# Even attention: the two softmaxes of a block joined on GpSimd in three operations, and a head's six epsilons in one

## The chip, the cores and the metric

The kernel runs on one core of a Trainium2 chip. The core has a matrix engine, TensorE (PE in the profile), which writes to PSUM; VectorE (DVE); ScalarE (ACT); and GpSimd (POOL), which reads and writes SBUF and not PSUM. SyncE (SP) issues most of the DMAs. Each engine works through its own instructions in a fixed order and waits on semaphores for the others. The metric is the device time of one execution in microseconds. The kernel before takes 1602.63 us, the median of three runs (1602.38 to 1602.99).

## What is computed

Two transformer layers over 512 tokens and 256 context tokens, width 1024, in fp32. The first layer's mixer ("even") is a gated chunk MLP beside a differential attention; the second's is a windowed attention with sinks; a SwiGLU follows each. The change lies in the differential attention, in which each of four heads has two sets of queries and keys of width 64 and values of width 128:

```python
def diff_attn(q, k, v, lam):
    ...
    s = jnp.einsum('bqhd,bkhd->bhqk', q, k).astype(jnp.float32) * ATTN_SCALE
    p = jax.nn.softmax(s, axis=-1).reshape(b, B_HEADS, 2, tq, tk)
    a = p[:, :, 0] - lam * p[:, :, 1]
    return jnp.einsum('bhqk,bkhe->bqhe', a.astype(v.dtype), v)

def diff_out(o, g, lam_init):
    b, t = o.shape[0], o.shape[1]
    return (rmsnorm(o, g) * (1.0 - lam_init)).reshape(b, t, B_V_WIDTH)
```

Token queries see all 768 keys, context queries only the 256 context keys. Since an RMS norm over the head's output follows, the kernel never divides by the first softmax's sum s0: it forms e0 - lam (s0 / s1) e1 from the two arrays of exponentials and their row sums s0 and s1, and puts EPS s0^2 into the norm in place of EPS.

## The kernel before

Matrices are split into a high and a low part ("hi", "lo") so that three fast matmuls make one of fp32 accuracy (`mm3`, L106 to L108). ScalarE makes the high part, VectorE or GpSimd subtracts it for the low one (`split`, L122 and L123; for weights `unit`, L81 and L84).

The even attention goes head by head, t = 0 to 3. `head(t)` calls `attend` for three pairs of blocks of 128 queries, qp = 0, 1, 2; the first two pairs are token queries with 768 keys ("long blocks"), the third is context queries with 256 ("short blocks"). `attend` calls `softmax_diff` for both blocks, then PE transposes the two joined arrays 128 columns at a time (L564), ScalarE and VectorE split them (L122, L123), three matmuls each multiply them with the values (L106 to L108), and ScalarE copies the output (L576).

In `softmax_diff`, for each of the two softmaxes c: scores on PE into a PSUM tile pw (L542, L543; two such tiles exist), the negated row maximum on VectorE (L544), the exponential with its row sum on ScalarE (L546) into an SBUF tile e (six exist). Then VectorE takes the reciprocal of s1 (L550), the factor -lam s0 / s1 (L551), the join e0 + factor e1 into e0 (L552), and the block's epsilon EPS s0^2 (L553).

Beside this, `head` does the previous head's norm in three steps (`norm`; the diagonal scalings are L173, the spreading matmuls L183, the product L609) and, in qp 1, stacks the next head's Q and K into hi and lo (`stack`: L261 and L262 on ScalarE and L265 for Q, L276 and L277 on ScalarE and L279 for K; L265 of the last head is on GpSimd, all other subtractions on VectorE).

Between the heads' matmuls PE has those of `gated(i)`, eight dense products for the gated MLP, into one PSUM tile pf, which ScalarE empties (L585). Their weights come through a ring: DMA by SyncE, high part on ScalarE (L81), low part on GpSimd (L84). In order of priority stand heads 0 and 1, then heads 2 and 3, with gated 4 to 7 and then `turn` and gated 0 to 3 behind them. The gelus of gated 4 to 7 (L632) stand on ScalarE behind the last exponential of head 1, and heads 2 and 3 on ScalarE behind these gelus; each change between the two functions costs a table load.

The order of the instructions on each engine isn't written by hand. The context `tile.TileContext(nc, schedule_with_timeline_sim=True)` plans it at build time from priorities and its own costs, and sets all semaphores. `issue_after` puts an instruction behind another one on the same engine.

Of the kernel before, what the change touches and what calls it, by code (L numbers as in the profile page):

```python
# [11 lines left out]
ALU = mybir.AluOpType  # L12
# [10 lines left out]
EPS = 1e-6  # L23
# [3 lines left out]
class Builder:  # L27
# [294 lines left out]
    def even(self):  # L322
        tc, nc, a = self.tc, self.nc, self.a
# [7 lines left out]
        def f3(tag="f3", bufs=8):  # L331
            return R1.tile([P, TA], F32, name=self.uid(tag), tag=tag, bufs=bufs)
# [4 lines left out]
        for k in range(0, KT, 2):  # L337
            t = self.load(Rh, a["xT"][k * P:(k + 2) * P, :].rearrange("(k p) t -> p k t", p=P), [P, 2, TX], f"hx{k}")
# [110 lines left out]
        for half, heads in enumerate(((0, 1), (2, 3))):  # L449
# [3 lines left out]
            for k in range(KT):  # L453
                t = self.adap.tile([P, 2, 512], F32R, name=self.uid("wq"), tag="wq", bufs=3) if k % 3 == 2 else None
# [8 lines left out]
                if half == 0:  # L463
                    t, sh = hx[k], self.modcol(0, 0, k, 0)
# [35 lines left out]
        for k in range(KT):  # L500
            W = self.unit(a["v0"][k * P:(k + 1) * P, :], 512)
            for tb in range(6):
                c = slice(tb * P, (tb + 1) * P)
# [24 lines left out]
        Ra = tc.alloc_tile_pool(name="att0", bufs=1, side="right", reuse_waits="tile")  # L528
        oraw, raw = [], {}

        def softmax_diff(Q, K, qb, eps):


            koff = 0 if qb < 4 else TX
            qs = slice(qb * P, (qb + 1) * P)
            nm, sums = self.small(2, "sa", 10), self.small(2, "sa", 10)
            es = []
            for c in range(2):
                ps = self.wide()
                for p in range(2):  # L540
                    if qb < 4:
                        nc.tensor.matmul(ps[:, :TX], Q[c][:, qs], K[c][p][:, :TX], start=p == 0, stop=p == 1)  # L542
                    nc.tensor.matmul(ps[:, TX:TA], Q[c][:, qs], K[c][p][:, TX:], start=p == 0, stop=p == 1)  # L543
                nc.vector.tensor_reduce(nm[:, c:c + 1], ps[:, koff:TA], axis=AX, op=ALU.max, negate=True)  # L544
                e = Ra.tile([P, TA], F32, name=self.uid("e"), tag="e", bufs=6)
                self.last_exp = nc.scalar.activation(e[:, koff:], ps[:, koff:TA], AF.Exp, bias=nm[:, c:c + 1],  # L546
                                                     accum_out=sums[:, c:c + 1])
                es.append(e[:, koff:])
            r = self.small(1, "sa", 10)
            nc.vector.reciprocal(r, sums[:, 1:2])  # L550
            nc.vector.scalar_tensor_tensor(r, r, self.nlam, sums[:, 0:1], ALU.mult, ALU.mult)  # L551
            nc.vector.scalar_tensor_tensor(es[0], es[1], r, es[0], ALU.mult, ALU.add)  # L552
            nc.vector.scalar_tensor_tensor(eps[:, qb:qb + 1], sums[:, 0:1], EPS, sums[:, 0:1], ALU.mult, ALU.mult)  # L553
            return es[0]

        def attend(t, Q, K, qp, o, eps):
            es = [softmax_diff(Q, K, 2 * qp + i, eps) for i in range(2)]
            kbs = list(range(6)) if qp < 2 else [4, 5]
            po = self.bank()[:, :TC]
            for i in range(0, len(kbs), 2):  # L560
                pt = self.bank()
                for j in range(2):
                    for b in range(2):
                        nc.tensor.transpose(pt[:, j * TC + b * P:j * TC + (b + 1) * P],  # L564
                                            es[b][:, (i + j) * P:(i + j + 1) * P], self.ident)
                th = Ra.tile([P, 512], F32R, name=self.uid("ath"), tag="at", bufs=6)
                tl = Ra.tile([P, 512], F32R, name=self.uid("atl"), tag="at", bufs=6)
                self.split(th, tl, pt)
                for j in range(2):
                    kb = kbs[i + j]  # L570
                    c = slice(t * P, (t + 1) * P)
                    m = slice(j * TC, (j + 1) * TC)
                    self.mm3(po, (vhi[kb][:, c], vlo[kb][:, c]), (th[:, m], tl[:, m]),
                             i + j == 0, i + j == len(kbs) - 1)
            s = slice(qp * TC, (qp + 1) * TC)
            nc.scalar.copy(o[:, s], po)  # L576
# [11 lines left out]
        def stack(t):  # L588
            return (self.stack_q(qk[t], Ra, TA, "sq", 3, eng=nc.gpsimd if t == 3 else nc.vector),
                    self.stack_k(qk[4 + t], Ra, TA, "sk", 6))  # L590
# [3 lines left out]
        def norm(t, step):  # L594

            if t not in norms:
                return
            o, eps = norms[t][:2]
            if step == 0:
                sq = self.sumsq()  # L600
                nc.scalar.activation(sq, o, AF.Square)
                norms[t] = o, eps, sq
            elif step == 1:
                sq = norms[t][2]
                norms[t] = o, eps, self.rstd_diag([(sq[:, :TX], TX), (sq[:, TX:], TC)], 1.0 / P, eps=eps)
            else:
                for off, T, dg in ((0, TX, norms[t][2][0]), (TX, TC, norms[t][2][1])):
                    c = o[:, off:off + T]
                    nc.vector.scalar_tensor_tensor(c, c, self.subg, self.spread(dg), ALU.mult, ALU.mult)  # L609

        def head(t):
            Q, K = QK.pop(t)
            o = f3("o", 4)
            eps = self.small(6, "sx", 2)
            for qp in range(3):
                attend(t, Q, K, qp, o, eps)
                if qp == 0:
                    norm(t - 1, 1)
                elif qp == 1:
                    if t < 3:  # L620
                        QK[t + 1] = stack(t + 1)
                    norm(t - 1, 2)
            norms[t] = o, eps
            norm(t, 0)
            if t == 3:
                norm(t, 1)
                norm(t, 2)
            oraw.append(o)
# [40 lines left out]
        for t in range(2):  # L669
            head(t)  # L670
# [5 lines left out]
        with tc.high_priority(offset=tc.cur_priority - here), tc.issue_after(last.ins):  # L676
            head(2)
            head(3)
# [889 lines left out]
```

## Time and profile before

| | us |
|---|---|
| median of three runs | 1602.63 |
| the profiled execution | 1600.63 |
| its span | 1598.8 |
| PE busy | 1522.4 |
| DVE busy | 1066.6 |
| POOL busy | 833.9 |
| ACT busy | 724.5 |

The profile shows one execution. Its span runs from the first to the last instruction of the trace; the rest of its time lies around that. Times of a trace are microseconds from the span's start. The four heads of the even attention run from 168 to 304 us; the rest of the span lies outside what is edited.

How lines are read: a group has line, engine, operation, out<-in, shapes and count, then busy time and mean nanoseconds of one, then the idle time of the engine just before them and what ended it. In a view of one line the three numbers are shortest, median and longest. In the chain of work that ended last each piece is followed back to what released it, so that the shares by line show what set the time; "issue" is time in which the engine waited for nothing that the profile shows. PEclk is the clock that TensorE was granted, as a share of the full one.

### The profile page before, as it was taken

Reading aid. Unit: us, or ns where it says so; the run is one execution under the profiler, and the core shown is the slowest. Engines: PE = TensorE matmul, PEld = TensorE weight load, DVE = VectorE, ACT = ScalarE, POOL = GpSimd, SP = SyncE. Lnnn points to the kernel's source line nnn. Section 1 sums busy time; section 2 is a strip of 40 time slices with the busy share of each in tenths; the row PEclk is TensorE's granted clock in tenths of the full one; section 3 lists DMA queues with packets and bytes.
Section 4 is the critical chain, followed back from the end, with each engine's and each line's share of the span. In section 5 each row is a group of like instructions: output and inputs, shape, how many; then the busy total and the mean of one; then the engine's idle time right before and its main releaser. Section 6 shows DMA issues by size and latency. Waiting matters only on the chain.

```text
span 1598.8 us, 24991 instructions
## 1 busy us (share of the span) xinstructions
PE 1522.4 (95%) x9547; PEld 1356.4 (85%) x9547; DVE 1066.6 (67%) x1956; ACT 724.5 (45%) x1472; POOL 833.9 (52%) x567
## 2 busy tenths in 40 slices
PE   6999988999989999999999989999999899999996
PEld 4676876889989999999999978777869899999996
DVE  4620788765687787878774485665667866666656
ACT  2422676553543333333333244565655645444442
POOL 0463211061256776777676415541304399888883
PEclk9999999999999999999999999999999999999998
DMA  8845100033233333454541012110225132323201
GB/s 326 306 139 191 40 8 1 14 127 124 67 98 107 112 99 123 153 156 147 162 156 48 27 52 80 60 34 14 67 80 204 52 111 97 113 86 113 93 14 54
DMA packets 54296, 162.01 MB, mean 101 GB/s; under 512 B 6176, under 2 KB 10656, under 8 KB 46496
## 3 DMA queue, kind: packets, MB, share of 16 engines
q1 hardware_dynamic: 47120, 135.11, 25.1%
q10 hardware_dynamic: 7056, 25.30, 5.0%
q8 instruction: 75, 1.23, 0.3%
q14 instruction: 45, 0.37, 0.1%
HBM read 158.29 MB, written 2.10 MB: 100 GB/s over the span
## 4 chain that ended last, share of the span: by engine, by line
PE 84%; DVE 9%; ACT 4%; issue 2%; DMA 1%; POOL 0%; POOLq 0%; SPq 0%; DVEq 0%; ACTq 0%
PE pw L107 11%; PE pw L106 11%; PE pw L108 11%; PE pb L107 8%; PE pb L106 8%; PE pb L108 8%; PE pf L106 4%; PE pf L107 4%; PE pf L108 4%; PE pb L1421 2%; PE pb L1410 2%; PE pf L359 2%; PE pw L1373 1%; PE pw L1381 1%; PE pw L542 1%
## 5 line engine op out<-in xcount | busy, mean ns | idle before, releaser
L84 POOL TENSOR_TENSOR w<-raw,w 128x512 fp32r<-128x512 f32 (+1 forms) x84 | 126.8, 1517 | 244.0 <-ACT w L81 221.9
L107 PE MATMUL pw<-ax,w 128*128 128x384 f32 (+2 forms) x732 | 234.0, 320 | 5.2 <-DVE ax L201 2.7
L774 DVE SCALAR_TENSOR_TENSOR xT<-pb,mod,xT 128x512 f32<-128x512 f32 (+3 forms) x208 | 146.0, 707 | 133.2 <-PE pb L108 132.7
L106 PE MATMUL pw<-ax,w 128*128 128x384 f32 (+2 forms) x732 | 232.7, 321 | 2.1 <-ACT ax L200 1.6
L108 PE MATMUL pw<-ax,w 128*128 128x384 f32 (+2 forms) x732 | 233.4, 320 | 0.1
L879 POOL TENSOR_TENSOR w<-t,w 128x512 fp32r<-128x512 f32 x100 | 152.8, 1531 | 58.8 <-ACT w L879 56.9
L879 POOL TENSOR_TENSOR w<-raw,w 128x512 fp32r<-128x512 f32 x110 | 166.6, 1530 | 23.3 <-ACT w L879 23.2
L106 PE MATMUL pb<-hh,w 128*128 128x512 f32 x480 | 171.3, 357 | 3.5 <-DVE xT L774 3.5
L108 PE MATMUL pb<-hh,w 128*128 128x512 f32 x480 | 171.7, 358 | 0.0
L107 PE MATMUL pb<-hh,w 128*128 128x512 f32 x480 | 171.3, 357 | 0.0
L106 PE MATMUL pw<-T,w 128*128 128x384 f32 (+1 forms) x508 | 157.0, 311 | 2.1 <-DVE hs L879 2.1
L107 PE MATMUL pw<-T,w 128*128 128x384 f32 (+1 forms) x508 | 157.7, 311 | 1.2 <-DVE T L123 1.2
L108 PE MATMUL pw<-T,w 128*128 128x384 f32 (+1 forms) x508 | 157.7, 311 | 0.0
L106 PE MATMUL pf<-ax,w 128*128 128x256 f32 (+2 forms) x420 | 140.4, 334 | 10.2 <-DVE qf L252 5.7
L107 PEld LDWEIGHTS pw<-ax,w 128*128 128x128 f32 x732 | 139.3, 190 | 12.5 <-DVE ax L201 3.6
L106 PEld LDWEIGHTS pw<-ax,w 128*128 128x128 f32 x732 | 138.7, 190 | 9.8 <-ACT ax L200 2.4
L108 PE MATMUL pf<-ax,w 128*128 128x256 f32 (+2 forms) x420 | 139.6, 332 | 3.2 <-DVE w L879 3.2
L108 PEld LDWEIGHTS pw<-ax,w 128*128 128x128 f32 x732 | 139.5, 191 | 3.1 <-DVE w L948 0.4
L107 PE MATMUL pf<-ax,w 128*128 128x256 f32 (+2 forms) x420 | 139.1, 331 | 0.0
L879 POOL TENSOR_TENSOR w<-rawo,w 128x512 fp32r<-128x512 f32 x60 | 104.9, 1749 | 32.6 <-ACT w L879 26.1
L879 POOL TENSOR_TENSOR hh<-hs,hh 128x512 fp32r<-128x512 f32 (+1 forms) x41 | 76.7, 1873 | 85.3 <-ACT hh L879 83.9
L228 DVE SCALAR_TENSOR_TENSOR junk<-ar,cb 128x1024 bf16<-128x1024 f32 x64 | 105.0, 1641 | 1.5 <-DMA ar<-ada 1.5
(380 smaller groups left out, 3926.1 us busy)
## 6 DMA issues: line engine op xcount, KB each, us to landing
raw<-ffn_in SPq DMA_DIRECT2D x44, 1024.0 KB, 5.2
ar<-ada SPq DMA_DIRECT2D x24, 1024.0 KB, 7.1
ar<-ada ACTq DMA_DIRECT2D x48, 512.0 KB, 3.6
rawo<-ffn_out SPq DMA_DIRECT2D x88, 256.0 KB, 3.0
raw<-odd_out SPq DMA_DIRECT2D x32, 256.0 KB, 2.7
raw<-qk SPq DMA_DIRECT2D x16, 256.0 KB, 8.5
raw<-uv SPq DMA_DIRECT2D x16, 256.0 KB, 2.8
raw<-even_out SPq DMA_DIRECT2D x8, 512.0 KB, 4.1
```

The source lines that it names most:

```text
L84: eng.tensor_tensor(lo, raw, hi.bitcast(F32), ALU.subtract)
L106: mm(out, s[0], m[0], start=start, stop=False, **kw)
L107: mm(out, s[0], m[1], start=False, stop=False, **kw)
L108: return mm(out, s[1], m[0], start=False, stop=stop, **kw)
L228: return self.nc.vector.scalar_tensor_tensor(junk, t, 1.0, self.cb[who], ALU.mult, ALU.mult, accum_out=self.acc[who][:, col:col + 1])
L359: nc.tensor.matmul(ps[32 * q:32 * q + 32, :w], cst[:, k, :], t[:, w * q:w * q + w], start=k == 0, stop=k == KT - 1, skip_group_check=True)
L542: nc.tensor.matmul(ps[:, :TX], Q[c][:, qs], K[c][p][:, :TX], start=p == 0, stop=p == 1)
L774: ins = self.nc.vector.scalar_tensor_tensor(h, ps[:, r], self.modcol(l, j, m, who), h, ALU.mult, ALU.add)
L879: tail[key] = fn(*args, **kw)
L1373: nc.tensor.matmul(ps[:, st:en], Q, K[g][p][:, b0 * P:b1 * P], start=p == 0, stop=p == 1, skip_group_check=True)
L1410: last = nc.tensor.transpose(pt[:, x * P:(x + 1) * P], es[2 * (x % 2) + x // 2][:, kb * P:(kb + 1) * P], self.ident)
L1421: nc.tensor.matmul(po[64 * h:64 * h + 64, :], V[vb][:, 64 * g:64 * g + 64], t[:, h * TC:h * TC + TC], start=kb == 0, stop=kb == nb - 1, sk ...
```

## The change

```diff
-        def softmax_diff(Q, K, qb, eps):
+        def softmax_diff(Q, K, qb, s0):
...
-            nm, sums = self.small(2, "sa", 10), self.small(2, "sa", 10)
+            nm, s1 = self.small(2, "sa", 10), self.small(1, "sa", 10)
+            sums = [s0[:, qb:qb + 1], s1]
...
                 self.last_exp = nc.scalar.activation(e[:, koff:], ps[:, koff:TA], AF.Exp, bias=nm[:, c:c + 1],
-                                                     accum_out=sums[:, c:c + 1])
+                                                     accum_out=sums[c])
                 es.append(e[:, koff:])
             r = self.small(1, "sa", 10)
-            nc.vector.reciprocal(r, sums[:, 1:2])
-            nc.vector.scalar_tensor_tensor(r, r, self.nlam, sums[:, 0:1], ALU.mult, ALU.mult)
-            nc.vector.scalar_tensor_tensor(es[0], es[1], r, es[0], ALU.mult, ALU.add)
-            nc.vector.scalar_tensor_tensor(eps[:, qb:qb + 1], sums[:, 0:1], EPS, sums[:, 0:1], ALU.mult, ALU.mult)
+            po = nc.gpsimd
+            nc.vector.reciprocal(r, s1)
+            po.tensor_scalar(r, r, self.nlam, sums[0], ALU.mult, ALU.mult)
+            po.tensor_scalar(es[1], es[1], r, None, ALU.mult)
+            po.tensor_tensor(es[0], es[0], es[1], ALU.add)
             return es[0]
...
         def head(t):
             Q, K = QK.pop(t)
             o = f3("o", 4)
-            eps = self.small(6, "sx", 2)
+            s0, eps = self.small(6, "sx", 4), self.small(6, "sx", 4)
             for qp in range(3):
-                attend(t, Q, K, qp, o, eps)
+                attend(t, Q, K, qp, o, s0)
...
+            nc.vector.scalar_tensor_tensor(eps, s0, EPS, s0, ALU.mult, ALU.mult)
             norms[t] = o, eps
```

The reciprocal of s1 stays on VectorE. The factor, the product of the second array with it (written in place) and the sum are three operations of GpSimd, where one operation of VectorE made the factor and one the join. The first softmaxes' sums of a head's six blocks are written by ScalarE side by side into one tile s0, a column each; behind the head's last block one VectorE operation makes all six epsilons from it.

## The prediction

> **What bounds the kernel now.** The page comes first. TensorE (PE) is busy nearly the whole span, the chain of work that ended last runs 84% over it, and VectorE (DVE) stands next with 9%.
>
> ```profile
> span 1598.8 us, 24991 instructions
> ...
> PE 1522.4 (95%) x9547; PEld 1356.4 (85%) x9547; DVE 1066.6 (67%) x1956; ACT 724.5 (45%) x1472; POOL 833.9 (52%) x567
> ...
> PE 84%; DVE 9%; ACT 4%; issue 2%; DMA 1%; POOL 0%; POOLq 0%; SPq 0%; DVEq 0%; ACTq 0%
> ```
>
> So the edit, all of it in the even attention, can win only idle time of PE there. Busy time by stretch shows where that is. Behind stretch and length stand PE, PEld, DVE, ACT and POOL, then the granted clock, the DMA share and GB/s; the last row holds all four heads.
>
> ```profile
> 170.00:194.00 24.00, 24.00 (x148) 21.46 (x149) 16.08 (x28) 13.04 (x27) 6.66 (x4) 1.00 0.16 50
> 194.00:210.00 16.00, 12.69 (x88) 11.14 (x88) 14.00 (x27) 12.26 (x26) 1.29 (x1) 1.00 0.02 3
> 229.00:250.00 21.00, 14.48 (x63) 11.77 (x63) 19.36 (x54) 16.44 (x28) 1.80 (x1) 0.76 0.00 0
> 264.00:276.00 12.00, 9.26 (x71) 8.38 (x70) 11.83 (x35) 8.65 (x20) 3.82 (x3) 1.00 0.00 1
> 276.00:310.00 34.00, 33.84 (x223) 30.12 (x222) 28.26 (x94) 21.04 (x44) 0.00 (x0) 1.00 0.00 1
> ...
> 168.00:304.00 136.00, 122.06 (x752) 106.61 (x751) 111.42 (x275) 90.76 (x187) 19.35 (x13) 0.96 0.04 13
> ```
>
> PE has three holes: A (194 to 210, 16.00 - 12.69 = 3.31 us idle), B (229 to 250, 6.52 us, at a clock of 0.76) and C (264 to 276, 2.74 us). In each DVE is nearly full, 88, 92 and 99%, while GpSimd (POOL) is busy 19.35 of the 136 us. Where there is no hole, the matmuls of `gated` fill PE between those of a head. I then read the last chain by line in three windows about the holes: 194 to 206, 226 to 252, and 264 to 272.5.
>
> ```profile
> by line: ACT e L546 16.9%; DVE sa L544 9.2%; ACT kh L277 7.0%; PE pb L107 6.2%; ACT kh L276 6.1%; ACT qa L261 5.3%; PE pf L106 5.2%; DVE atl L123 5.1%; ACT f L585 5.0%; PE pb L564 4.7%; DVE e L552 4.0%; PE pb L108 3.9%; ACT ath L122 3.9%; i
> ...
> by line: ACT e L546 11.3%; ACT f L632 11.1%; PE pw L542 7.9%; DVE kl L279 7.4%; ACT kh L276 6.0%; PE pw L543 5.4%; issue 5.2%; DVE atl L123 5.0%; ACT L632 4.9%; ACT L546 4.9%; ACT ath L122 4.1%; DVE qb L265 3.7%; PE pb L156 3.4%; PE pb L183
> ...
> by line: DVE e L552 32.9%; DVE kl L279 22.5%; DVE atl L123 14.1%; DVE sa L544 11.4%; DVE stats L648 9.5%; DVE sx L553 6.2%; DVE sa L551 5.0%; DVE mv L649 3.8%; DVE sa L550 2.8%; DVE sm L166 2.4%; issue 1.8%
> ```
>
> C is made by DVE alone, and the join (L552), the factor (L551) and the epsilon (L553) are 32.9 + 5.0 + 6.2 = 44.1% of its 8.5 us, 3.75 us. In A the join is 4.0% of 12 us, 0.48 us. In B it is not on the chain: there stand the stacking of the next head's Q and K (L276, L279, L265), gelus (L632) and two table loads (the bare L632 and L546).
>
> **What leaves DVE.** Busy us and mean ns of the groups in 168 to 304:
>
> ```profile
> L552 DVE SCALAR_TENSOR_TENSOR e<-e,sa,e 128x768 f32<-128x768 f32 x16 | 17.3, 1083 | 0.3
> ...
> L552 DVE SCALAR_TENSOR_TENSOR e<-e,sa,e 128x256 f32<-128x256 f32 x8 | 6.0, 744 | 0.0
> ...
> L551 DVE SCALAR_TENSOR_TENSOR sa<-sa,nlam,sa 128x1 f32<-128x1 f32 x24 | 5.1, 213 | 0.3
> ...
> L553 DVE SCALAR_TENSOR_TENSOR sx<-sa 128x1 f32<-128x1 f32 x24 | 4.7, 195 | 2.0 <-ACT e L546 1.9
> ```
>
> That is 17.3 + 6.0 + 5.1 + 4.7 = 33.1 us. The epsilons come back as 4 operations on 128x6; at L553's 195 ns, 0.8 us. DVE loses 32.3 us and keeps 79 of 136.
>
> **What POOL takes.** No row of before has POOL multiply by a column, so I bound it by its neighbours; the three numbers are shortest, median and longest ns.
>
> ```profile
> L123 POOL TENSOR_TENSOR ax<-o,ax x14: 725/734/1832, 327.9 to 1200.2; 128x256 fp32r<-128x256 f32 x12, 128x768 fp32r<-128x768 f32 x2
> ...
> L123 POOL TENSOR_TENSOR hh<-hs,hh x1: 2795/2795/2795, 469.9 to 469.9; 128x768 fp32r<-128x768 f32 x1
> ...
> L1428 POOL COPY pt<-rc x8: 611/612/617, 1044.4 to 1190.5; 128x512 f32<-128x512 f32 x8
> ```
>
> The add on 768 columns: 1.8 to 2.8 us, taken 2.0, nearer the calm row, since DVE will have less to do beside it. The multiply has one wide input like the copy: at least 612 x 1.5 = 0.9 us, at most the add's calm 1.8; taken 1.1. The factor: L551's 0.2, from zero to twice that. A long block (768): 3.3 us (2.7 to 5.0). A short one (256): 0.2 + 1.1/3 + 0.73 = 1.3 us (1.0 to 2.1, with a third of each long end and the factor's). In all 16 x 3.3 + 8 x 1.3 = 63 us, so POOL goes to 82 of 136; at the upper ends to 97 + 19 = 116. Throughput doesn't bind it. No DMA is added and none moves on SP's or POOL's queue.
>
> **What gets later.** The joined array is ready 3.3 us after the reciprocal instead of 0.21 + 1.08 = 1.3: +2.0 us (1.4 to 3.7) for a long block, and +0.4 (1.3 - 0.21 - 0.74) for a short one. Behind a waiting factor on POOL stand the rest of the join and the low parts of the gate weights (L84), for which gated matmuls wait; behind a waiting transpose (L564) on PE stands all PE work. The second e tile of a block is freed 2.0 us later as well; with six such tiles the next block's two exponentials have theirs, and the third may wait. What covers the 2.0 us is the filler, and for heads 0 and 1 it ends here:
>
> ```profile
> 225.37 0.28 PE L108 MATMUL pf<-ax,w 128*128 128x256 f32 x1
> ```
>
> B lies behind that. There I charge half of one +2.0, since the next head's scores hide some: +1.0 us (0 to 3.7).
>
> **The sum.** A: the join's 0.48 leaves the chain, -0.5 (0 to -3.3, the hole). B: two short joins with factor and epsilon are 2 x (0.74 + 0.21 + 0.20) = 2.3 us of DVE in a stretch where it is 92% busy; the stacks stay on the chain but stand behind less: 2.3 x 0.92 = -2.1 (0 to -6.5). C: 3.75 us leave a chain whose hole is 2.74, after which PE is the limit: -2.7 (0 to -2.7). Lost cover: +1.0. Together -4.3 us. The profiled execution took 1600.63 us, its span of 1598.8 and 1.8 around it, so it would take 1596.3; it lies 2.0 under the median of 1602.63, so the median goes to 1598.3. Every term has zero as an end because the planner orders each engine anew from its own costs, and the filler may stand otherwise about every join.
>
> **A rule that speaks against it.** Rows of DVE, and then of POOL, in order of time: one long join beside a POOL subtraction, six diagonal scalings beside another, and six of these alone.
>
> ```profile
> 223.12 2.12 DVE L552 SCALAR_TENSOR_TENSOR e<-e,sa,e 128x768 f32<-128x768 f32 x1
> ...
> 240.27 2.86 DVE L173 TENSOR_SCALAR q<-ident,sm 128x128 f32<-128x128 f32 x6
> ...
> 325.07 1.27 DVE L173 TENSOR_SCALAR q<-ident,sm 128x128 f32<-128x128 f32 x6
> ```
>
> ```profile
> 223.14 1.29 POOL L84 TENSOR_TENSOR w<-raw,w 128x512 fp32r<-128x512 f32 x1 [10.74 <-ACT w L81]
> ...
> 240.85 1.80 POOL L265 TENSOR_TENSOR qa<-f,qa 64x768 fp32r<-64x768 f32 x1 [12.90 <-ACT qa L261]
> ```
>
> The join took 2.12 against the group's mean of 1.08, so 1.0 us more; the scalings 2.86 against 1.27, so 1.6 more. The Trainium skill, page "SBUF — State Buffer", section "Who interferes with whom", says that a VectorE instruction with two SBUF inputs contends with a GpSimd instruction that reads SBUF, and that one in a two-port mode is shut out for the whole of it. By that rule, the rows agree; what it makes of the time is the first rival.
>
> **The rivals.** *Blocked VectorE (slower).* With POOL busy 82 of 136 us, the stacking (two inputs in SBUF, 7.4% of 26 us or two pieces of 0.96 in B) and the scalings meet POOL's adds as those rows did. A meeting costs a stacking piece 0.9 us at the join's ratio, and a norm 1.6. On B's chain lie three pieces (L279 twice, L265 once) and a norm, 2.7 + 1.6; on C's two pieces, 1.8; with one long block's full lateness in each, 2 x 2.0, this is +10.1. Against it stand the gains of A to C, 5.3: +4.8, so 1607.4 us. It decides once the joins of a head run beside the stacks of the next. For it: a stack is issued right behind a pair of long blocks, whose joins then run. Against: the reductions (L544) read PSUM, and the splits (L123) have one operand there; these are most of what stays on DVE.
>
> *Absorbed.* A and C close, but B is held by ScalarE's gelus and table loads, and the ends of heads 1 and 3 each lose 1.0: -3.2 + 2.0 = -1.2, so 1601.4 us. For it: three of B's four largest entries off PE (e L546, f L632, kh L276) are ScalarE's.
>
> *The paced join.* POOL costs the upper 5.0 us a long block, and the last long block of each head is seen in full: 4 x 3.7 = 14.8 less 5.3, so 1612.1 us. Against: filler stands behind heads 0 and 2.
>
> That the change doesn't do what it says is no rival: each epsilon is taken from the same sum, column by column.
>
> **How the numbers follow.** Forecast 0.45 (own range 1592 to 1599.4, the lower end with B mostly closed), absorbed 0.20, blocked 0.29, paced 0.06. A measurement of this kernel can tell about 0.2% from no change, 3.2 us, so "same" is 1599.4 to 1605.8. Faster 0.45; same 0.20; slower 0.29 + 0.06 = 0.35. The range for 8 in 10 runs from 1591.5 (A, C and most of B gone, -11) to 1609 (blocked, and 1.6 us more for a second norm met).
>
> **What would show it.** Right: DVE busy near 79 us in the heads' stretch and POOL near 82; C's 2.74 us of idle gone; POOL adds near 2.0 us and multiplies near 1.1; stacking pieces still near 0.96. Wrong: PE waiting for POOL at L564 by more than 2 us in all; stacking pieces and scalings half again as long; B longer than now; or a difference made beyond 400 us, where nothing is edited.

## The result, and the profile after

The changed kernel takes 1611.09 us, the median of six runs (1610.18 to 1611.52); the kernel before, run beside it, 1602.51 (1600.45 to 1602.99). The ratio is 1.0061, with a 95% interval of 1.0050 to 1.0072: slower by some 9 us, where 4.3 us of gain were forecast. The profiled execution took 1611.52 us.

The page of the changed kernel, its head and its shares of the chain that ended last:

```profile
span 1609.7 us, 25064 instructions
...
PE 1528.3 (95%) x9547; PEld 1361.7 (85%) x9547; DVE 1050.4 (65%) x1888; ACT 724.8 (45%) x1472; POOL 918.1 (57%) x639
...
PE 83%; DVE 7%; ACT 4%; issue 2%; POOL 2%; DMA 1%; POOLq 0%; SPq 0%; DVEq 0%; ACTq 0%
```

POOL has 2% of the last chain, where it had none. The span grew by 10.9 us. Where that happened is seen from single lines of the two kernels (shortest, median, longest ns; then first and last start). The exponentials and the projection's residuals, before:

```profile
L546 ACT ACTIVATE e<-pw,sa x48: 454/902/938, 172.0 to 301.1; 128x768 f32<-128x768 f32 x32, 128x256 f32<-128x256 f32 x16
...
L774 DVE SCALAR_TENSOR_TENSOR xT<-pb,mod,xT x208: 339/751/753, 370.0 to 1582.9; 128x512 f32<-128x512 f32 x88, 128x256 f32<-128x256 f32 x12, 128x384 f32<-128x384 f32 x2, 128x128 f32<-128x128 f32 x2
```

and after, where three lines have been added above the second:

```profile
L547 ACT ACTIVATE e<-pw,sa x48: 453/900/917, 172.2 to 312.6; 128x768 f32<-128x768 f32 x32, 128x256 f32<-128x256 f32 x16
...
L777 DVE SCALAR_TENSOR_TENSOR xT<-pb,mod,xT x208: 339/751/752, 380.9 to 1593.8; 128x512 f32<-128x512 f32 x88, 128x256 f32<-128x256 f32 x12, 128x384 f32<-128x384 f32 x2, 128x128 f32<-128x128 f32 x2
```

The last exponential of the four heads starts 11.5 us later, the first residual behind them 10.9 us and the last residual of the kernel 10.9 us. Everything is lost inside the heads, nothing beyond 400 us. Busy time over the heads and in the stretch ahead of B, before, and then after (stretch and length; PE, PEld, DVE, ACT, POOL; granted clock, DMA share, GB/s):

```profile
168.00:301.60 133.60, 119.66 (x742) 104.68 (x741) 109.24 (x263) 88.39 (x184) 19.35 (x13) 0.96 0.04 13
...
210.00:229.00 19.00, 18.65 (x126) 16.55 (x124) 13.70 (x25) 12.15 (x27) 4.64 (x3) 1.00 0.04 13
```

```profile
168.00:313.10 145.10, 127.13 (x750) 110.55 (x748) 91.73 (x194) 88.45 (x183) 101.98 (x81) 0.91 0.04 12
...
194.00:211.00 17.00, 13.53 (x78) 12.06 (x77) 13.66 (x19) 11.68 (x24) 10.57 (x10) 0.80 0.03 10
211.00:238.00 27.00, 23.15 (x153) 20.23 (x151) 16.19 (x28) 17.48 (x39) 23.26 (x18) 1.00 0.04 10
238.00:254.00 16.00, 10.00 (x42) 8.10 (x43) 12.61 (x35) 13.69 (x22) 8.27 (x8) 0.57 0.00 0
...
266.00:273.90 7.90, 7.90 (x69) 7.77 (x68) 4.23 (x7) 7.44 (x15) 6.75 (x6) 1.00 0.00 0
273.90:277.70 3.80, 0.55 (x5) 0.36 (x4) 3.76 (x4) 1.37 (x4) 2.60 (x2) 0.89 0.01 2
277.70:283.00 5.30, 5.02 (x20) 4.46 (x21) 3.75 (x24) 2.37 (x7) 2.87 (x5) 0.50 0.01 3
```

The heads are 11.5 us longer: PE's idle time rose from 13.94 to 17.97 us (length less busy), 4.0 us; its busy time rose by 7.5 us for nearly the same matmuls (750 for 742), most of it because they ran at a lower clock. The holes are still there, A (194 to 211) with 3.5 us idle, B (238 to 254) with 6.0, C (273.9 to 277.7) with 3.25; together they are 12.7 us, and before 12.6. What is new is that DVE is no longer full in A (80%), that the clock is down to 0.80 in A and 0.57 in B (before, 1.00 and 0.76), and that POOL is 86% busy ahead of B, from 211 to 238. There PE idles 3.85 us, against 0.35 us from 210 to 229 before, which is most of the 4.0 us. POOL's groups show why it is so busy (busy us, mean ns, idle before and its releasers):

```profile
L554 POOL TENSOR_SCALAR e<-e,sa 128x768 f32<-128x768 f32 x16 | 35.5, 2221 | 1.0
L555 POOL TENSOR_TENSOR e<-e,e 128x768 f32<-128x768 f32 x16 | 29.6, 1852 | 0.6
L84 POOL TENSOR_TENSOR w<-raw,w 128x512 fp32r<-128x512 f32 x12 | 16.0, 1343 | 8.7 <-ACT w L81 8.7
...
L553 POOL TENSOR_SCALAR sa<-sa,nlam,sx 128x1 f32<-128x1 f32 x24 | 8.2, 342 | 40.8 <-DVE sa L552 30.6 <-ACT ath L122 4.2 <-DVE mv L652 2.7
```

The multiply by a column takes 2.22 us, longer than the add of two arrays (1.85), and twice the forecast's 1.1. A long join is 0.34 + 2.22 + 1.85 = 4.4 us. The chain that ended last, from 211 to 238.5, by line and some of its pieces (start, us, what):

```profile
by line: POOL e L554 36.2%; POOL e L555 22.5%; issue 15.6%; POOL w L84 13.7%; POOL sa L553 6.1%; ACT e L547 5.7%; ACT f L587 1.0%; POOLq L554 0.3%; POOLq L84 0.2%
...
224.46 1.83 POOL e L554
...
226.63 2.51 POOL w L84 x2
229.15 1.80 POOL e L555
230.94 0.32 POOL sa L553
...
232.18 3.71 POOL e L554 x2
235.89 2.06 POOL e L555
...
237.97 0.57 ACT e L547 x2
```

The chain goes from join to join on POOL from 212.5 to 238; POOL's operations are 78.5% of the window. Two subtractions for gate weights (L84) stand inside a join, between its multiply and its add. At the end an exponential (L547) waits for the e tile that the add frees. At C it is another engine that is late. The group of the stacking pieces before, in 168 to 304, and the two pieces at C after, as the chain shows them one by one:

```profile
L279 DVE TENSOR_TENSOR kl<-f,kh 64x768 fp32r<-64x768 f32 x10 | 9.5, 952 | 0.2
```

```profile
272.45 2.46 DVE kl L279
274.93 2.47 DVE kl L279
```

DVE there, in order of time, then POOL and PE ("[3.28 <-" is the idle time before, and its releaser):

```profile
272.45 4.94 DVE L279 TENSOR_TENSOR kl<-f,kh 64x768 fp32r<-64x768 f32 x2
277.42 0.16 DVE L166 SCALAR_TENSOR_TENSOR sm<-pb,sx 128x4 f32<-128x4 f32 x1
```

```profile
272.25 1.85 POOL L555 TENSOR_TENSOR e<-e,e 128x768 f32<-128x768 f32 x1
274.17 2.40 POOL L265 TENSOR_TENSOR qb<-f,qb 64x768 fp32r<-64x768 f32 x1
```

```profile
277.73 0.45 PE L566 MATMUL pb<-ident,e 128*128 128x128 f32 x1 [3.28 <-DVE sm L166]
277.83 0.56 PE L544 MATMUL pw<-kh,qb 128*128 128x256 f32 x1
...
278.40 0.84 PE L566 MATMUL pb<-ident,e 128*128 128x128 f32 x3
```

Two stacking pieces took 4.94 us; before, their mean was 0.95 us a piece. Each lies beside one POOL operation with two SBUF operands that had started before it, and ended 0.8 us after that one: POOL's ended at 274.10 and 276.57, the pieces at 274.91 and 277.40. So a piece stood until POOL was through, and its price is what is left of POOL's operation. PE waits 3.28 us for the small DVE operation behind them. So both a paced join (ahead of B) and a blocked VectorE (at C) are in the trace. Which of them costs the time is what the runs were for.

### The profile page after: what moved, and what is told of

Its sections match the earlier page's. It is cut to its first block, busy times and chain, and to the rows that moved or that the text cites. A ratio compares the mean times of both kernels' runs of the same rounds, so it can differ in the third digit from the quotient of the medians.

```text
span 1609.7 us, 25064 instructions
## 1 busy us (share of the span) xinstructions
PE 1528.3 (95%) x9547; PEld 1361.7 (85%) x9547; DVE 1050.4 (65%) x1888; ACT 724.8 (45%) x1472; POOL 918.1 (57%) x639
## 4 chain that ended last, share of the span: by engine, by line
PE 83%; DVE 7%; ACT 4%; issue 2%; POOL 2%; DMA 1%; POOLq 0%; SPq 0%; DVEq 0%; ACTq 0%
PE pw L106 11%; PE pw L107 11%; PE pw L108 11%; PE pb L106 8%; PE pb L108 8%; PE pb L107 8%; PE pf L106 4%; PE pf L107 4%; PE pf L108 4%; PE pb L1424 2%; PE pb L1413 2%; PE pf L359 2%; PE pw L1376 1%; PE pw L1384 1%; PE pw L384 1%
## 5 line engine op out<-in xcount | busy, mean ns | idle before, releaser
L84 POOL TENSOR_TENSOR w<-raw,w 128x512 fp32r<-128x512 f32 (+1 forms) x84 | 124.7, 1491 | 171.1 <-ACT w L81 169.6
```

The costliest lines, as they stand in the source:

```text
L84: eng.tensor_tensor(lo, raw, hi.bitcast(F32), ALU.subtract)
```

## The experiments

Four theories stand in the expectations. *Paced*: the join's 4.4 us on POOL set the pace. *Blocked*: POOL's reads hold up DVE operations with two SBUF operands. *Queue*: POOL's other work stands between the joins, and behind them. *Order*: the planner's new order of all engines, made from its own costs, does the harm. All ratios below are to the kernel before run beside the experiment; its medians there were 1601.73 us (first four), 1602.25 (e5 to e8), 1600.43 (e9 to e12) and 1600.60 (e13 to e16). Diffs are against the changed kernel unless another is named.

**Is it the join at all?** The epsilon part alone, with the join as before on DVE:

```diff
-            po.tensor_scalar(r, r, self.nlam, sums[0], ALU.mult, ALU.mult)
-            po.tensor_scalar(es[1], es[1], r, None, ALU.mult)
-            po.tensor_tensor(es[0], es[0], es[1], ALU.add)
+            nc.vector.scalar_tensor_tensor(r, r, self.nlam, sums[0], ALU.mult, ALU.mult)
+            nc.vector.scalar_tensor_tensor(es[0], es[1], r, es[0], ALU.mult, ALU.add)
```

> The sums in one tile and the six epsilons in one operation as in the changed kernel; factor and join stay on VectorE as before. Paced (the joined array comes 3.1 us later, 0.34 + 2.22 + 1.85 of GpSimd against 0.21 + 1.08 of VectorE, and the heads wait for it) and blocked (GpSimd's reads slow VectorE's two-input work, the stacking pieces from 0.95 to 2.47 us beside its adds) both expect no loss: VectorE does 4 us less, 1599 to 1603 us. Order (the planner's new order or the shared tile of sums costs the time, not GpSimd) expects a good part of the 8.6 us: 1606 us or more.

Measured: 1603.26 us, 1.0007 (0.9998 to 1.0016). The epsilons cost nothing that can be told; the loss is the join's.

The join on POOL in every other block:

```diff
+            if qb % 2 == 0:
...
+            else:
+                nc.vector.scalar_tensor_tensor(r, r, self.nlam, sums[0], ALU.mult, ALU.mult)
+                nc.vector.scalar_tensor_tensor(es[0], es[1], r, es[0], ALU.mult, ALU.add)
```

> The changed kernel with the join of only the first block of each pair on GpSimd; the second block's factor and join are on VectorE. The first block's 4.4 us then lie under the second block's two reductions and exponentials. Paced expects nearly all the loss gone: 1599 to 1604 us, stacking pieces may still be long. Blocked expects half the reads and half the loss: 1606 to 1607 us. Order expects no rule, anywhere up to 1611.

Measured: 1604.81 us, 1.0025 (1.0015 to 1.0035), about 40% of the loss for half of the joins: the loss goes about with their number, and lies between what *paced* and what *blocked* had for it. The joins left on DVE took longer beside POOL's, 1.33 us instead of 1.08:

```profile
L559 DVE SCALAR_TENSOR_TENSOR e<-e,sa,e 128x768 f32<-128x768 f32 x8 | 10.7, 1333 | 0.2
```

**How long may a join be on POOL?** First the multiply cut to one column, then, instead, the add; the other columns are left unscaled, or without the second softmax:

```diff
-            po.tensor_scalar(es[1], es[1], r, None, ALU.mult)
+            po.tensor_scalar(es[1][:, :1], es[1][:, :1], r, None, ALU.mult)
```

> The changed kernel with GpSimd's multiply cut to the first of its columns; the scaling of the other columns of the second array is left out. The join costs GpSimd about 0.34 + 0.35 + 1.85 = 2.5 us instead of 4.4, so it is 1.2 us later than VectorE's instead of 3.1. Paced expects the loss to shrink with it, 8.6 x 1.2 / 3.1 = 3.3: about 1606 us (1603 to 1607). Blocked expects the adds, the two-input reads, to keep most of it: 1608 to 1610 us.

```diff
-            po.tensor_tensor(es[0], es[0], es[1], ALU.add)
+            po.tensor_tensor(es[0][:, :1], es[0][:, :1], es[1][:, :1], ALU.add)
```

> The changed kernel with GpSimd's add cut to the first of its columns; the second softmax is left out of the other columns. The join takes GpSimd 0.34 + 2.22 + 0.3 = 2.9 us, 1.6 us later than VectorE's join, and it reads one input only. Paced, drawn as a line through the multiply cut to one column (1.2 us late, -0.24%) and the changed kernel (3.1 us late, +0.61%), expects near -0.06%: 1599 to 1602 us. Blocked, by which only two-input reads hurt, expects less than the multiply cut gave: 1595 us or less.

Measured: 1596.91 us, 0.9976 (0.9966 to 0.9986), and 1603.19 us, 1.0015 (1.0006 to 1.0025). Both fell outside what *paced* and *blocked* had for them, the first below both and the second above both. With the multiply cut, POOL's group of it in that kernel is

```profile
L554 POOL TENSOR_SCALAR e<-e,sa 128x1 f32<-128x1 f32 x24 | 7.4, 310 | 2.1
```

so a long join is 0.34 + 0.31 + 1.85 = 2.5 us, and the same change of place is then a gain of 0.24%. The other columns of the multiply, 1.9 us in each of 16 long blocks, turn that into a loss of 0.61%, the planner's new order included.

Then the same product in another form, the factor on DVE and the column spread over the array as a second operand:

```diff
-            po.tensor_scalar(r, r, self.nlam, sums[0], ALU.mult, ALU.mult)
-            po.tensor_scalar(es[1], es[1], r, None, ALU.mult)
+            nc.vector.scalar_tensor_tensor(r, r, self.nlam, sums[0], ALU.mult, ALU.mult)
+            po.tensor_tensor(es[1], es[1], r.to_broadcast([P, es[1].shape[-1]]), ALU.mult)
```

> Complete. The changed kernel with the factor on VectorE and GpSimd's multiply as a product of two arrays, the second a column repeated: if it costs what the add costs, GpSimd has 1.85 + 1.85 = 3.7 us a long block instead of 4.4, and reads two inputs in both. Paced and queue expect a loss between the changed kernel's 8.6 and zero, near that of the late chain (3.6 us on GpSimd, +0.16%): 1603 to 1607 us. Blocked expects more than the changed kernel's, since both operations now read twice: 1611 us or more.

Measured: 1605.21 us, 1.0030 (1.0018 to 1.0041). Its POOL groups, and DVE at C:

```profile
L555 POOL TENSOR_TENSOR e<-e,e 128x768 f32<-128x768 f32 x16 | 29.5, 1843 | 1.0
L554 POOL TENSOR_TENSOR e<-e,sa 128x768 f32<-128x768 f32 x16 | 23.5, 1467 | 32.3 <-DVE sa L553 19.1 <-ACT w L81 7.9 <-PE pf L108 2.7
```

```profile
269.81 4.38 DVE L279 TENSOR_TENSOR kl<-f,kh 64x768 fp32r<-64x768 f32 x2
```

The product in this form takes 1.47 us, and POOL's part of a long join 1.47 + 1.84 = 3.3 us, which is the forecast's own price for it. The loss halves but stays a loss, as *paced* and *queue* expected; *blocked* had expected more than the changed kernel's. POOL is gone from the first places of the chain over the heads, and the two stacking pieces at C are still stretched, 4.38 us. It isn't the join that holds them there: POOL subtracts for the gates (L84, from 269.60 to 270.88) and then for the last head's Q (L265, from 271.34 to 273.37), and the pieces end 0.8 us behind each, at 271.70 and 274.18. So a join of the price forecast would not have given the time forecast.

**Blocked VectorE.** The low part of K made from one SBUF operand, as K times 0, so that the stacking of K has no second one, and K's low part is left out of the scores; first with the join of 4.4 us, then with the one of 3.3 us:

```diff
-                nc.vector.tensor_tensor(kl[Z], k[X], kh[X].bitcast(F32), ALU.subtract)
+                if tag == "sk":
+                    nc.vector.tensor_scalar(kl[Z], k[X], 0.0, None, ALU.mult, ALU.add, accum_out=self.small(1, "ka", 2)[Z])
+                else:
+                    nc.vector.tensor_tensor(kl[Z], k[X], kh[X].bitcast(F32), ALU.subtract)
```

> The changed kernel with the low parts of the stacked keys made by an operation with one SBUF input that also writes a sum (K's low part is left out of the scores). If GpSimd's reads no longer stretch these pieces, they stay near 0.95 us where two of them took 2.47 each. Blocked expects most of the loss gone, 1605 us or less. Paced and queue expect 2 to 4 us back, the stall at that one place: 1606 to 1609 us.

> e10 with the low parts of the stacked keys made by an operation with one SBUF input (K's low part is left out of the scores). Blocked expects e10's loss of 0.30% mostly gone: 1603 us or less. Paced (lateness of 3.3 us blocks) expects it to stay: 1604 to 1608 us.

Measured: 1610.74 us, 1.0066 (1.0050 to 1.0081), and 1598.83 us, 0.9988 (0.9979 to 0.9998). In the second kernel the pieces are not stretched:

```profile
L280 DVE TENSOR_SCALAR_CACHE_REDUCE kl<-f 64x768 fp32r<-64x768 f32 x12 | 11.3, 945 | 0.5 <-PE pw L547 0.3
```

At 4.4 us a join, freeing the stacking changes nothing, where *blocked*, *paced* and *queue* had all expected some of the loss back: something else is as late. At 3.3 us it turns +0.30% into -0.12%, where *paced* had expected the loss to stay. That is more than the pieces alone had lost: the 16 of e10 took 18.7 us, 3.6 more than at 945 ns each, and 0.42% is 6.7 us. How much of the rest is the clock behind the holes, and how much a new order, isn't shown. By the Trainium skill, page "SBUF — State Buffer", section "Who interferes with whom", a DVE operation with at most one SBUF operand, outside the two-port modes, isn't held; the pieces agree, with 945 ns beside a POOL that was busy 78.3 us in the heads, against 79.9 in the kernel that stretched them. The prediction put the same section's rule on the two-port modes too simply: there the one that starts first holds the other up, whichever engine it is on.

**Latency alone, and traffic alone.** Against the kernel before: POOL does a factor, a product and a sum of nearly the join's size (632 columns of a constant), and nothing waits for them; then nothing of that, but behind DVE's join POOL makes a small product, fills a scratch tile five times (twice in a short block) and makes another small product that the transposes wait for:

```diff
+            rg, po = self.small(1, "sg", 2), nc.gpsimd
+            po.tensor_scalar(rg, r, self.nlam, self.nlam, ALU.mult, ALU.mult)
...
+            po.tensor_scalar(w, c, rg, None, ALU.mult)
+            po.tensor_tensor(w, c, w, ALU.add)
```

> The kernel before, its joins on VectorE, and beside each GpSimd does a factor, a multiply and an add from a constant array into a scratch array of 632 (long) or 256 (short) columns, for which nobody waits. Same reads and the same queue in front of the gate weights, 82% of the columns, no lateness. Blocked expects most of the loss: 1608 us or more, and with the joins themselves slowed perhaps more than the changed kernel. Paced expects 1601 to 1605 us, with stacking pieces long where they meet GpSimd.

```diff
+            po.tensor_tensor(gh[:, :1], x[:, :1], self.ones[:, :1], ALU.mult)
+            for _ in range(5 if qb < 4 else 2):
+                po.memset(gh, 1.0)
+            po.tensor_tensor(x[:, 1:2], x[:, 1:2], gh[:, 1:2], ALU.mult)
```

> The kernel before, its joins and epsilons on VectorE; behind each join GpSimd does a chain that reads one column, fills a scratch array of 632 columns five times (long block, some 3 us) or twice (short), and touches one column of the joined array, so that the transposes wait for it. Lateness near the changed kernel's, almost nothing read from SBUF, VectorE with all its work. Paced expects the loss of the changed kernel or more: 1608 to 1614 us. Blocked expects 1601 to 1604 us.

Measured: 1603.03 us, 1.0014 (1.0005 to 1.0024), and 1603.92 us, 1.0016 (1.0006 to 1.0027). The groups of the first and of the second:

```profile
L556 POOL TENSOR_SCALAR gh<-sguT,sg 128x632 f32<-128x632 f32 x16 | 32.5, 2030 | 1.4
L557 POOL TENSOR_TENSOR gh<-sguT,gh 128x632 f32<-128x632 f32 x16 | 25.2, 1574 | 0.9
```

```profile
L557 POOL MEMSET gh<- 128x632 f32 x96 | 60.1, 626 | 5.2
L558 POOL TENSOR_TENSOR e<-e,gh 128x1 f32<-128x1 f32 x24 | 7.2, 300 | 1.9
```

Traffic of 2.03 + 1.57 us a long block without a wait costs 0.14%. A delay of 5 x 0.63 + 0.3 and a first product, some 3.6 us, without that traffic costs 0.16%. Neither is the loss, and both together would be half of it, although these two kernels keep the join's whole time on DVE as well. So *blocked* missed in the first and *paced* in the second, where it had expected 1608 to 1614 us. The second fills POOL's queue too, so lateness and a full queue without reads aren't the loss either. Neither kernel has lateness and reads at once, and neither holds the second e tile until POOL's add is through; which of these makes the rest isn't shown.

**The queue.** The gates' low parts and the last head's Q stack on DVE instead of POOL, with the join of 4.4 us and with that of 3.3 us:

```diff
+            self.dve_lo = 1
             W = self.blocks(a["uv"][i])
+            self.dve_lo = 0
...
-            return (self.stack_q(qk[t], Ra, TA, "sq", 3, eng=nc.gpsimd if t == 3 else nc.vector),
+            return (self.stack_q(qk[t], Ra, TA, "sq", 3, eng=nc.vector),
```

> The changed kernel with the low parts of the gate weights, which stand between the joins in GpSimd's queue (1.3 us each), and the two stacking pieces of the last head on VectorE. The joins keep their 4.4 us. Queue (GpSimd's backlog, joins standing behind each other and behind other work, makes the loss) expects at least 3 us back: 1603 to 1608 us. If the join's own length or the blocking of VectorE makes it: 1609 to 1613 us.

> Complete. e10 with the low parts of the gate weights and the last head's stacking on VectorE. Queue expects about the 0.2% back that this gave in the changed kernel: 1601 to 1603 us. If lateness of the single join is what is left: 1605 to 1607 us.

Measured: 1606.72 us, 1.0041 (1.0026 to 1.0056), and 1603.06 us, 1.0016 (1.0004 to 1.0028). An emptier queue gives back a third of the loss in the first pair and about half in the second, though the intervals of each pair touch or overlap.

**Less work on POOL.** The factor on DVE; the multiply on DVE, on ACT, and in turns on both; the add on POOL:

```diff
...
-            po.tensor_scalar(es[1], es[1], r, None, ALU.mult)
+            nc.vector.tensor_scalar(es[1], es[1], r, None, ALU.mult)
```

> Complete. Factor and multiply on VectorE, the add alone on GpSimd: 0.21 + 0.55 to 1.0 + 1.85 us, 1.3 to 1.8 us later than before, VectorE gives up nothing to half of a join. Paced expects 1599 to 1603 us. If what counted in the multiply cut to one column was VectorE's 32 us and not the shorter join, more: 1603 to 1606 us.

```diff
...
-            po.tensor_scalar(es[1], es[1], r, None, ALU.mult)
+            nc.scalar.mul(es[1], es[1], r)
```

> Complete. Factor on VectorE, multiply on ScalarE (some 0.85 us for a long block), add on GpSimd: 0.21 + 0.85 + 1.85 = 2.9 us, 1.6 us later than before, and VectorE keeps none of the join. Paced expects 1598 to 1602 us unless ScalarE, which gets 16 x 0.85 + 8 x 0.45 = 17 us more in a stretch where it is 67% busy, becomes the next one late: then 1603 to 1607 us, with the wait for ScalarE's splits grown.

```diff
...
+            if qb % 2 == 0:
+                nc.scalar.mul(es[1], es[1], r)
+            else:
+                nc.vector.tensor_scalar(es[1], es[1], r, None, ALU.mult)
```

> Complete. Factor on VectorE; the multiply on ScalarE for the first block of a pair and on VectorE for the second; the add on GpSimd, 1.85 us. Both engines keep room, as each has half of what made e7 (-0.08%) and e8 (-0.05%). Paced expects 1597 to 1600 us; if the planner's order scatters results by some 2 us whatever is done, 1598 to 1603.

Measured: 1600.06 us, 0.9992 (0.9983 to 1.0000); 1600.96 us, 0.9995 (0.9986 to 1.0003); 1600.81 us, 0.9999 (0.9989 to 1.0008). Each takes the product's 2.2 us off POOL, and with them the loss; what is left is no gain that can be told, although DVE is relieved as well. DVE's product, in the first of them:

```profile
L554 DVE TENSOR_SCALAR e<-e,sa 128x768 f32<-128x768 f32 x16 | 11.8, 736 | 0.7
```

Last, both engines on one join: DVE joins the first 512 columns and POOL the last 256, or DVE 256 and POOL 512 with the product in the second form; a short block is DVE's in both, and so is the factor. The first of them:

```diff
...
+            c = 512 if qb < 4 else 256
+            nc.vector.scalar_tensor_tensor(es[0][:, :c], es[1][:, :c], r, es[0][:, :c], ALU.mult, ALU.add)
+            if qb < 4:
+                po.tensor_scalar(es[1][:, c:], es[1][:, c:], r, None, ALU.mult)
+                po.tensor_tensor(es[0][:, c:], es[0][:, c:], es[1][:, c:], ALU.add)
```

> Complete. VectorE joins the first 512 columns of a long block and all of a short one; GpSimd multiplies and adds the last 256 columns, which are transposed last, in 0.92 + 0.73 = 1.7 us. Paced expects the lateness hidden behind the first two groups of transposes and a small gain from VectorE's 16 x 0.27 + 4 us: 1598 to 1602 us. Blocked expects a third of the reads and 1604 us.

> Complete. VectorE joins the first 256 columns of a block, GpSimd the other 512 of a long block by a product of two arrays and an add, 1.0 + 1.25 = 2.3 us, near the 2.5 us of the multiply cut to one column, and VectorE gives up about 16 x 0.55 + 4 = 13 us instead of 32. Paced expects 1597 to 1601 us; blocked 1603 us or more.

Measured: 1601.63 us, 1.0008 (0.9997 to 1.0020), and 1603.39 us, 1.0017 (1.0006 to 1.0027). Sharing a join between the two engines doesn't pay either, at either cut.

By POOL's time for a long join, from the groups of each kernel:

| POOL's us a long join | what else | ratio to before |
|---|---|---|
| 4.4 | the change | 1.0061 |
| 4.4 | K's low part from one operand | 1.0066 |
| 4.4 | queue emptied | 1.0041 |
| 3.3 | factor on DVE | 1.0030 |
| 3.3 | the same, queue emptied | 1.0016 |
| 3.3 | the same, K's low part from one operand | 0.9988 |
| 2.8 | add cut | 1.0015 |
| 2.5 | multiply cut | 0.9976 |
| 2.4 | DVE joins 256 columns of 768 | 1.0017 |
| 2.0 | DVE joins 512 columns of 768 | 1.0008 |
| 1.85 | multiply on DVE, ACT, or both | 0.9992, 0.9995, 0.9999 |

The trend is plain, and so is its scatter: 2.8 and 2.5 us give signs that differ. Each version gets an order of its own from the planner, so that a change of 2 us or so between versions may be order's; no run held the order fixed, and this stays open. The kernel before itself ranged from 1595.74 to 1604.04 us beside the last four, the shorter times at the higher mean granted clock (0.982 to 0.989), so that only medians of many executions can be compared here. No version that computes everything is faster than the kernel before by more than 0.2%, and none was found that beats it clearly. The two that do, at -0.24% and -0.12%, leave work out; what the relief of DVE alone is worth isn't shown.

## Why the prediction was wrong

The forecast of 1598.3 us fell, and 1611.09 lies outside its range. Two steps failed, the price of the multiply and the stacking pieces taken as unchanged, and a third term, the clock, had been put at nothing.

**The price of the multiply.** The step "taken 1.1", with the bounds 0.9 to 1.8 from POOL's copy and its add, was mis-sized: it measured 2.22 us, above both. The bound "at most the add's calm 1.8" supposed that an operation with one wide operand can't be slower than one with two. So a long block took 4.4 us, not 3.3, and POOL's 82 of 136 became 102 of 145. That is still no bound by throughput over the whole, as the prediction said, but it is one from 211 to 238, where POOL was 23.26 of 27 us busy. The paced join, with a chance of 0.06, gave 1612.1 us for 5.0 us a block. That its time nearly came out is partly luck: it counted one late block in full at the end of each head, and the trace has a chain of joins from 211 to 238 and a lower clock, while the late chain without reads, 3.6 us a block, cost only 0.16%. The argument against it, "filler stands behind heads 0 and 2", overlooked that the low parts for this filler stand in the same queue. With the multiply cut to one column the sign turns, and with it off POOL the loss goes; at the price forecast, half of the loss stays.

**The stacking pieces.** With the price forecast, 3.3 us, the time was still 0.30% above before. There "stacking pieces still near 0.96" failed: two at C took 4.38 us, and with K's low part from one operand the loss went. That is the blocked VectorE, given 0.29, though more came back than the pieces alone had lost. Its 0.9 us a meeting was too small: at C in the changed kernel the two cost 4.94 - 2 x 0.95 = 3.0 us, not 1.8, since a piece stands for as long as POOL's operation still runs. In the changed kernel itself it wasn't the only limit, since freeing the pieces gained nothing there. Its prediction of 1607.4 us had the mechanism of a kernel with a cheaper multiply (measured 1605.21).

**The clock.** The sum counted idle time of PE and no change of its clock. In the heads the clock stood at 0.50 for 10.2 us before (231.6 to 238.4 and 245.2 to 248.7) and for 27.3 us after (201.8 to 208.6, 239.3 to 253.0 and 276.8 to 283.7). PE's busy time at this clock rose from 9.1 to 19.5 us; half of the difference, 5.2 us, is an estimate of what the half clock added to the heads, beside 4.0 us more of idle time. It doesn't decide alone: with the multiply cut to one column the half clock lasted 20.5 us in the heads of the profiled execution, and that kernel is faster than the one before.

**Point by point.** *What leaves DVE*: 32.3 us were to go and 79 to stay; 91.73 stayed, over the longer stretch. The groups of the join, the factor and the epsilons did go, but the stacking of K gave back 5.9 us, the four epsilon operations took 0.81 us each instead of 0.195, and busy times of neighbouring DVE instructions overlap (the groups before sum to 124 us where DVE was busy 111.42), so that groups can't be subtracted from a busy time one for one:

```profile
L279 DVE TENSOR_TENSOR kl<-f,kh 64x768 fp32r<-64x768 f32 x10 | 15.4, 1540 | 1.2 <-ACT kh L276 1.0
L625 DVE SCALAR_TENSOR_TENSOR sx<-sx 128x6 f32<-128x6 f32 x4 | 3.2, 812 | 0.7 <-ACT e L547 0.7
```

*The add*: 2.0 forecast, 1.85 measured. *The factor*: 0.2 forecast with 0.4 as the upper end, 0.34 measured. *The gain at A*: half a microsecond was to leave; the hole holds 3.5 us. *At C*: 2.74 us were to close; 3.25 us are there, made by other work of DVE than before. *B*: of the gain of 2.1 there is 0.5, with 6.0 us of idle time for 6.52, and the clock fell from 0.76 to 0.57. *The lost cover*, put at 1.0 with 3.7 as its end, is 3.5 us of added idle time ahead of B, beside POOL's chain. *Lateness*: +2.0 us a block was 4.4 - 1.3 = +3.1, inside its bounds of 1.4 to 3.7; only the charge for it, half of one block in the whole kernel, was far too small, since consecutive joins queue behind each other. *PE waiting for POOL at L564* by more than 2 us was named as a sign; there is one such wait, 1.9 us (the line is L566 after the change). PE's other waits are for ACT and DVE, and POOL's part in them is seen only in the chain. *Nothing beyond 400 us* held, and the epsilons alone cost nothing.

What stays open: how the 0.61% divides between the pace, the blocking, the clock and the order. Traffic alone (0.14%) and latency alone (0.16%) don't add up to it, and the versions in between each have their own order. Nor did a run give the join more than six e tiles, though in the changed kernel exponentials waited 2.4 us for POOL's add and 4.0 us for transposes, where the profile before has no such wait.

## What to carry to other kernels

Price an operation by its own form on its own engine; an operation with fewer operands isn't always the cheaper one, and if no row shows the form, the upper bound must lie above the neighbours. An engine that is idle on average isn't free for a piece on the path between two others: its latency enters the chain, whatever stands in its queue enters with it, and a run with that operand cut to one column tells what its price makes of the time. Count the clock behind a hole, and not only the hole. Before work goes to GpSimd, look for what DVE does with two SBUF operands at that time, and who waits for it.

## What the runs showed of the hardware

GpSimd's product of a 128x768 array with a column took 2.22 us as a scaling by a column (TENSOR_SCALAR) and 1.47 us as a product of two arrays, the second being the column spread out (TENSOR_TENSOR); the sum of two real arrays took 1.85 us. With a single column the first form took 0.31 us, so its time lies in the columns, 2.5 ns each.

A DVE operation with two SBUF operands that started beside a running POOL operation with two stood until that one's end: the stacking pieces at C ended 0.8 us after POOL's operations, and took 2.46 and 2.47 us instead of 0.95. A piece that ran from 233.17 to 234.13, while POOL multiplied by a column (232.16 to 234.36), took 0.95 us as ever.

An idle gap cost more than its length. PE stood still for 3.28 us at C, and in the 5.30 us behind it the granted clock was 0.50. The kernel before had it at B, where the gap was shorter:

```profile
232.63 0.58 PE L543 MATMUL pw<-kh,qb 128*128 128x256 f32 x1 [2.53 <-ACT e L546]
```

```profile
233.00:236.00 3.00, 2.90 (x11) 2.31 (x11) 2.97 (x11) 2.02 (x7) 0.00 (x0) 0.50 0.00 0
```

The Trainium skill, page "TensorE: Matmul & The Clock Gate", section "What's actually happening", has TensorE fall to half its clock after an idle window of about 3.4 us that runs on its own time. The half clock agrees, and so do its stretches in the heads of both kernels, 3.4, 6.8 or 13.7 us long, one, two or four such windows. But it came after gaps of 3.28 us and of 2.53 us, so a gap clearly shorter than that figure was enough. The gap's length alone doesn't tell it either: behind one of 2.68 us that ended at 242.88 in the kernel before, the clock was still full until 245.2. In the changed kernel the heads lost most of 7.5 us to slower matmuls, beside 4.0 us of idle time.
